# Moving the first block's residual gate into the last block, as seven products in turn between W_A and W_B

## The chip, the cores and the metric

The kernel runs on one core of a Trainium2 chip. The metric is the device time of one execution in microseconds; the median of three runs before the change is 2507.09 us (2506.99 to 2508.43).

## What is computed

One layer of a hybrid sequence model over 2048 prompt tokens and 64 sample tokens, width 1024, all in float32. What matters for this change is the end of the layer; the reference cut to it:

```python
merged = jax.nn.sigmoid(gA) * yA + jax.nn.sigmoid(gB) * yB      # yA = a @ w_a_out, yB = o @ w_b_out
out = jnp.einsum('btd,de->bte', merged, w_o)
x = x + rms_norm(out, g_post)
gate = jax.nn.sigmoid(jnp.einsum('btd,de->bte', rms_norm(x, g_ple), w_ple_gate))
x = x + jnp.einsum('btp,pd->btd', p.astype(x.dtype), w_ple_proj) * gate
```

In the kernel `h` is `rms_norm(x, g_ple)`, `p` is the product with `w_ple_proj`, and the last two lines are "the gate" or W_G.

## The kernel before

The tokens lie along the free dimension, in three blocks of 768, 704 and 640 tokens (`SIZES`, line 35); the width of 1024 is 8 tiles of 128 partitions. A block runs through `path_b` (attention heads), `path_a` (a gated convolution), and then four square products with 1024 x 1024 weights: W_A, W_B, W_O and W_G (line 33). Between W_O and W_G stands the normalization `final_norm` (line 1420).

**Three matmuls for one.** Each operand is split into a rounded part `hi` and the rest `lo` (`split`, line 229: ScalarE casts, VectorE subtracts), and each product is hi x hi + hi x lo + lo x hi (lines 457 to 459, 608 to 610, 645 to 647).

**Plain products.** `gemm` (line 652) makes one output tile from 8 k in two halves of the tokens, 24 matmuls each half. `final_gate` (line 1497) does W_G so for the first and the second block: 8 outputs; for each it asks for x and p from DRAM (`reload`), takes the sigmoid on ScalarE, multiplies and adds on VectorE, and stores y.

**Seven products in turn.** `in_turn` (line 573) makes a square product from 2 x 2 quarters with seven products in place of eight (`IN_TURN`, line 84). The quarters of the weights are A11, A12, A22 and the sums S1 to S4; those of the operand are B11, B21, B22 and the sums T1 to T4, made in place by VectorE (`operand_of`, line 555). Each product has four units `g` of 12 matmuls, each unit with one weight tile of 128 x 512. A unit's operand for the next product is prepared during the present one (`lead`, 1). The result of a quarter goes to a `sink`: the first column's upper quarter after A12, then after A22, S1 and S4. Before the change this form does W_A and W_O of the first block, W_A, W_B and W_O of the other two, and W_G of the last (`gate_in_turn`, line 1514).

**Weights.** `load_raw` (line 238) brings a tile of 256 KB on SP's queue, five in flight. `split_w` (line 269) splits it anew, or loads its `lo` from DRAM if an earlier use has stored it; `used_later` (line 255) says which are stored. From the second block on these stores go on POOL's queue (`stores`, line 1677). The sums S1 to S4 are made beforehand and kept in DRAM with their low parts (`prepare_sums`, line 375); those of W_G are made in the last block's `path_b`.

**Order and room.** The order of the work is that of the Python program, with weights at high priority and small steps hung between products by hand (`hooks`, `spread_out`, line 1530). `paced` (line 306) makes a DMA wait for the latest matmul. All activations live in one ring of 48 tiles in SBUF (`rt`, line 155). `keep_h` (line 1478) stores h to DRAM, and `ask_h` (line 1482) brings the second block's back during the last block's W_O, since the second block's gate runs after the last block's W_O. `merge_in_turn` (line 1360) sets up W_A and W_B in turn, with a list of what is loaded after which product.

Of the kernel before, what the change touches and what calls it, by code (L numbers as in the profile page):

```python
# [13 lines left out]
AF = mybir.ActivationFunctionType  # L14
# [80 lines left out]
def hybrid_step(  # L95
# [159 lines left out]
    def used_later(idx, part):  # L255

        if GA * 8 <= idx < GB * 8 + KB - 2:
            return part in ("S1", "S2", "S3", "S4")  # L260
        if idx in (GB * 8 + KB - 1, IV * 8):
            return part != 0 and (part != 1 or idx >= GA * 8)
        if idx < GA * 8:
            return part != 1
        if W_B <= idx < W_O:
            return part == 1 and idx - W_B >= KH
        return True
# [305 lines left out]
    def in_turn(stages, operand, lead=1):  # L573
# [5 lines left out]

        def prepare(i, k):  # L580
            if i < len(todo):
                st, n = todo[i]
                late = st["order"] is IN_TURN_LATE
                made.setdefault(i, []).append(operand_of(st["raw"], st["order"][n][1], k, late))
# [4 lines left out]
        for i, (st, n) in enumerate(todo):  # L589
            block, _, what = st["order"][n]  # L590
# [3 lines left out]
            for g in range(KH):  # L594
                i1, i2 = st["idx"] + g, st["idx"] + KH + g
                with tc.high_priority():
                    hi, lo = kept_w(i1, i2, block, block in st["anew"])
                start = what[0] != "c"
                if start:
                    other = what == "u2" and st["order"] is IN_TURN_LATE  # L600
                    st["bank"][g] = [ps_attn()[:, : hn()] if other else ps_gemm(), st["bank"].get(g)]
                ps, held = st["bank"][g]
                if what == "u2":
                    st["bank"][g] = held
                add = partial(T.matmul, ps, skip_group_check=not start)
                for k in range(KH):
                    xhi, xlo = xs[k]
                    add(hi[:, k, :], xhi, start=start and k == 0, stop=False)  # L608
                    add(hi[:, k, :], xlo, start=False, stop=False)  # L609
                    last[0] = add(lo[:, k, :], xhi, start=False, stop=k == KH - 1).ins  # L610
                if what == "p1":
                    st["mid"].append(rt())
                    with tc.high_priority():
                        A.copy(half(st["mid"][g], 0), ps)
                u2, p57 = half(st["mid"][g], 0), half(st["mid"][g], 1)
                if what == "c11":
                    st["sink"](g, 0, 0, ps, None)
                elif what == "u2":
                    V.tensor_tensor(u2, u2, ps, ALU.add)
                elif what == "c21":  # L620
                    st["sink"](g, 1, 0, u2, ps)
                elif what == "c12":
                    st["sink"](g, 0, 1, u2, ps)
                elif what in ("p5", "p7") and g not in st["other"]:
                    st["other"].add(g)
                    with tc.high_priority():
                        A.copy(p57, ps)
                elif what in ("p5", "p7"):
                    t = hf()
                    with tc.high_priority():  # L630
                        A.copy(t, ps)
                    V.tensor_tensor(p57, p57, t, ALU.add)
                    st["sink"](g, 1, 1, u2, p57)
# [726 lines left out]
    def merge_in_turn(a, kept, mg, first):  # L1360


        ob, m = [], []

# [11 lines left out]
        def loads(idx, n):  # L1376
# [4 lines left out]
                (W_A, 3): ("o", ob),  # L1381
                (W_A, 5): ("o", ob),
                (W_A, 6): (GB, mg),
                (W_B, 1): (GB, mg),
            }.get((idx, n), (None, m))
            if kind is not None:
# [449 lines left out]
```

## Time and profile before

| | us |
|---|---|
| median of 3 runs | 2507.09 |
| lowest, highest | 2506.99, 2508.43 |
| profiled execution: span | 2509.2 |
| first block's gate (L645 to L647, 128 x 384) | 959.6 to 1026.7 |
| last block: W_A, W_B, W_O in turn (L608 to L610) | 2222.1 to 2374.2 |
| second block's gate, with the last block's product of p | 2374.2 to 2452.7 |
| last block's gate in turn | 2452.7 to 2502.3 |

The span runs from the first to the last instruction of the one profiled execution; no other time is given for that execution. The stretches are read from the starts of the matmuls by line and number of columns. PE is TensorE's matmuls, PEld its weight loads, DVE is VectorE, ACT is ScalarE, POOL is GpSimd, whose queue issues the DMAs of activations (q0), and SP is SyncE, whose queue issues those of weights (q1).

### The profile page before, as it was taken

Reading aid. Unit: us, or ns where it says so; the run is one execution under the profiler, and the core shown is the slowest. Engines: PE = TensorE matmul, PEld = TensorE weight load, DVE = VectorE, ACT = ScalarE, POOL = GpSimd, SP = SyncE. Lnnn points to the kernel's source line nnn. Section 1 sums busy time; section 2 is a strip of 40 time slices with the busy share of each in tenths; the row PEclk is TensorE's granted clock in tenths of the full one; section 3 lists DMA queues with packets and bytes.
Section 4 is the critical chain, followed back from the end, with each engine's and each line's share of the span. In section 5 each row is a group of like instructions: output and inputs, shape, how many; then the busy total and the mean of one; then the engine's idle time right before and its main releaser. Section 6 shows DMA issues by size and latency. Waiting matters only on the chain.

```text
span 2509.2 us, 47311 instructions
## 1 busy us (share of the span) xinstructions
PE 2491.1 (99%) x16254; PEld 2474.0 (99%) x16254; DVE 1932.2 (77%) x3699; ACT 1503.9 (60%) x2926; POOL 513.9 (20%) x875
## 2 busy tenths in 40 slices
PE   9999999999999999999999999999999999999998
PEld 9999999999999999999999999999999999999998
DVE  7889999988868775588886657977677776678766
ACT  6676676554453664466655556576666655565646
POOL 2032223321022021122223211102122222111031
PEclk9999999999999999999999999999999999999999
DMA  8789888997697798788889988979988879889887
GB/s 330 241 302 336 320 297 318 331 321 271 229 339 259 250 329 295 258 270 287 283 278 332 337 293 307 327 266 357 349 284 289 278 257 313 297 274 337 294 302 259
DMA packets 344240, 746.14 MB, mean 297 GB/s; under 512 B 43318, under 2 KB 48496, under 8 KB 344000
## 3 DMA queue, kind: packets, MB, share of 16 engines
q1 hardware_dynamic: 287136, 519.96, 60.3%
q0 software_dynamic: 56864, 223.16, 25.1%
q8 instruction: 128, 2.10, 0.3%
q14 instruction: 112, 0.92, 0.1%
HBM read 530.59 MB, written 212.36 MB: 296 GB/s over the span
## 4 chain that ended last, share of the span: by engine, by line
PE 90%; DMA 3%; DVE 3%; ACT 2%; issue 1%; POOL 0%; SPq 0%; ACTq 0%; DVEq 0%; POOLq 0%
PE pg L457 20%; PE pg L458 19%; PE pg L459 19%; PE pg L609 5%; PE pg L608 5%; PE pg L610 5%; PE pg L646 3%; PE pg L647 3%; PE pg L645 3%; DMA raw<-S 2%; PE pa L1142 1%; PE pa L1110 1%; PE pa L1180 1%; PE pa L1182 1%; DMA raw<-w_blk 1%
## 5 line engine op out<-in xcount | busy, mean ns | idle before, releaser
L457 PE MATMUL pg<-r,hi 128*128 128x320 f32 (+2 forms) x3304 | 1074.7, 325 | 1.1 <-DVE r L505 1.1
L458 PE MATMUL pg<-r,hi 128*128 128x320 f32 (+2 forms) x3304 | 1066.8, 323 | 0.0
L459 PE MATMUL pg<-r,lo 128*128 128x384 f32 (+2 forms) x2380 | 775.3, 326 | 0.4 <-DMA lo<-low 0.4
L457 PEld LDWEIGHTS pg<-r,hi 128*128 128x128 f32 x3304 | 621.0, 188 | 3.5 <-DVE r L505 1.7
L458 PEld LDWEIGHTS pg<-r,hi 128*128 128x128 f32 x3304 | 621.6, 188 | 0.0
L279 ACT CAST hi<-raw 128x512 fp32r<-128x512 f32 x566 | 349.9, 620 | 415.4 <-PE pg L458 170.6
L459 PEld LDWEIGHTS pg<-r,lo 128*128 128x128 f32 x2380 | 447.1, 188 | 0.7 <-DMA lo<-low 0.7
L230 ACT CAST hi<-raw 128x512 fp32r<-128x512 f32 x404 | 249.5, 621 | 206.3 <-PE pg L458 83.8
L609 PE MATMUL pg<-r,hi 128*128 128x320 f32 (+2 forms) x976 | 312.1, 321 | 2.5 <-DVE r L230 2.5
L608 PE MATMUL pg<-r,hi 128*128 128x320 f32 (+2 forms) x976 | 309.8, 320 | 0.0
L459 PE MATMUL pg<-r,s 128*128 128x352 f32 (+1 forms) x924 | 291.4, 315 | 0.0
L230 DVE TENSOR_TENSOR lo<-raw,hi 128x512 fp32r<-128x512 f32 x304 | 208.1, 686 | 82.7 <-ACT hi L230 75.9
L230 DVE TENSOR_TENSOR r<-r,r 128x320 fp32r<-128x320 f32 (+7 forms) x374 | 220.2, 608 | 46.1 <-ACT r L230 44.9
L230 ACT CAST r<-r 128x320 fp32r<-128x320 f32 (+7 forms) x374 | 195.9, 557 | 35.0 <-DVE r L1353 9.0
L610 PE MATMUL pg<-r,lo 128*128 128x320 f32 (+2 forms) x640 | 204.2, 319 | 0.1
L609 PEld LDWEIGHTS pg<-r,hi 128*128 128x128 f32 x976 | 183.2, 188 | 4.6 <-DVE r L230 4.3
L608 PEld LDWEIGHTS pg<-r,hi 128*128 128x128 f32 x976 | 182.3, 188 | 1.4 <-ACT r L230 1.0
L230 ACT CAST hi<-s 128x512 fp32r<-128x512 f32 x164 | 101.9, 623 | 127.3 <-PE pg L458 97.0
L459 PEld LDWEIGHTS pg<-r,s 128*128 128x128 f32 x924 | 173.5, 188 | 0.0
L471 ACT COPY hf<-pg 128x352 f32<-128x352 f32 (+2 forms) x354 | 157.5, 448 | 0.8 <-PE pg L459 0.7
L230 DVE TENSOR_TENSOR lo<-s,hi 128x512 fp32r<-128x512 f32 x164 | 114.2, 696 | 45.6 <-ACT hi L230 43.1
L505 DVE TENSOR_TENSOR r<-hf,pg 128x128 f32<-128x128 f32 (+5 forms) x164 | 64.3, 411 | 98.7 <-PE pg L459 98.6
(389 smaller groups left out, 4223.4 us busy)
## 6 DMA issues: line engine op xcount, KB each, us to landing
raw<-w_blk SPq DMA_DIRECT2D x559, 256.0 KB, 4.6
raw<-S SPq DMA_DIRECT2D x452, 256.0 KB, 4.2
lo<-low SPq DMA_DIRECT2D x340, 256.0 KB, 4.4
s<-low SPq DMA_DIRECT2D x226, 256.0 KB, 5.1
low<-lo SPq DMA_DIRECT2D x207, 256.0 KB, 3.9
S<-s SPq DMA_DIRECT2D x152, 256.0 KB, 4.2
low<-r POOLq DMA_DIRECT2D x66, 256.0 KB, 4.5
r<-w_blk POOLq DMA_DIRECT2D x64, 256.0 KB, 6.7
```

Source lines behind the costliest of these rows:

```text
L230: return A.copy(hi, src).ins, V.tensor_tensor(lo, src, hi.bitcast(F32), ALU.subtract).ins
L279: A.copy(hi, raw)
L457: add(hi[:, k, :], xhi, start=start and k == 0, stop=False)
L458: add(hi[:, k, :], xlo, start=False, stop=False)
L459: last[0] = add(lo[:, k, :], xhi, start=False, stop=k == KH - 1).ins
L471: copied = A.copy(got[n], ps[bank])
L608: add(hi[:, k, :], xhi, start=start and k == 0, stop=False)
L609: add(hi[:, k, :], xlo, start=False, stop=False)
L610: last[0] = add(lo[:, k, :], xhi, start=False, stop=k == KH - 1).ins
L645: T.matmul(ps, hi[:, k % 4, :], xhi[:, c], start=k == ks[0], stop=False)
L646: T.matmul(ps, hi[:, k % 4, :], xlo[:, c], start=False, stop=False)
L647: last[0] = T.matmul(ps, lo[:, k % 4, :], xhi[:, c], start=False, stop=k == ks[-1]).ins
```

## The change

The first block no longer runs `final_gate`. Its h goes to DRAM as the second block's does (`keep_h`, and 0 for `early` in `final_norm`). A new stage `earlier_gate` stands in the last block's list of stages, between W_A and W_B, with the first block's width of 768 (`as_of`). Its h is asked for after the fourth and sixth product of W_A, its p and x as half tiles four places ahead, and what W_B loads after products of W_A is now loaded after those of the new stage. `used_later` leaves out the low part of W_G's A21, which only the second block's plain gate uses. The body of the loop in `in_turn` has become the function `unit`, without other change. The core of the diff:

```diff
@@ used_later
+        if idx >= W_G + KH:
+            return part == 1
         return True
@@ in_turn
+        def as_of(st):
+            return sized_to(st["bl"]) if "bl" in st else nullcontext()
...
-                made.setdefault(i, []).append(operand_of(st["raw"], st["order"][n][1], k, late))
+                with as_of(st):
+                    made.setdefault(i, []).append(operand_of(st["raw"], st["order"][n][1], k, late))
...
+                with as_of(st):
+                    unit(st, n, g, xs)
@@ merge_in_turn
-    def merge_in_turn(a, kept, mg, first):
+    def merge_in_turn(a, kept, mg, first, between=None):
+        by = W_G if between else W_A
...
-                (W_A, 3): ("o", ob),
-                (W_A, 5): ("o", ob),
-                (W_A, 6): (GB, mg),
+                (by, 3): ("o", ob),
+                (by, 5): ("o", ob),
+                (by, 6): (GB, mg),
...
+            if between and idx == W_A and n in (3, 5):
+                between["ask"]()
+            if between and (idx, n) == (W_A, 6):
+                between["terms"](4)
...
             dict(idx=W_A, order=IN_TURN, raw=a, sink=sink_a, anew=("A11", "A12")),
+            *([between] if between else []),
             dict(idx=W_B, order=IN_TURN, raw=ob, sink=sink_b, anew=("A11", "A12")),
@@ new
+    def earlier_gate(bl, kept):
+        h, asked = [], []
+        places = iter([(g, c, q) for c, q in ((0, 0), (1, 0), (1, 1), (0, 1)) for g in range(KH)])
+
+        def ask():
+            with sized_to(bl):
+                for j in range(len(h), len(h) + KH):
+                    h.append(reload(kept["h", j], True))
+
+        def ask_terms(n):
+            with sized_to(bl):
+                for g, c, q in islice(places, n):
+                    t = rt()
+                    for o, kind in enumerate("px"):
+                        paced(G.dma_start(half(t, o), half(kept[kind, g + c * KH], q)))
+                    asked.append(t)
+
+        def sink(g, c, q, x, y):
+            j, t, s = g + c * KH, asked.pop(0), whole(x, y)
+            if y is None:
+                s = hf()
+                A.activation(s, x, AF.Sigmoid)
+            else:
+                A.activation(s, s, AF.Sigmoid)
+            v = half(t, 0)
+            V.tensor_tensor(v, v, s, ALU.mult)
+            V.tensor_tensor(v, v, half(t, 1), ALU.add)
+            G.dma_start(y_fm[j * P : (j + 1) * P, bl["t0"] + q * hn() : bl["t0"] + (q + 1) * hn()], v)
+            ask_terms(1)
+
+        return dict(idx=W_G, order=IN_TURN, raw=h, anew=(), sink=sink, bl=bl, ask=ask, terms=ask_terms)
@@ main loop
+        between = earlier_gate(blocks[0], kepts[0]) if bl["last"] else None
+        before, loads, ob, m = merge_in_turn(a, kept, mg, first, between)
...
-            norm = sized(bl, final_norm(bl, xo, kept, partial(split_h, h2) if first else partial(keep_h, kept), int(first)))
+            norm = sized(bl, final_norm(bl, xo, kept, partial(keep_h, kept), 0))
...
-            if first:
-                run(final_gate(bl, h2, kept))
-            else:
+            if not first:
```

More of the change, by code (lines that the diff above doesn't have):

```diff
@@ L589, in in_turn @@
         for i, (st, n) in enumerate(todo):
-            block, _, what = st["order"][n]
             if n == 0:
@@ L594, in in_turn @@
             for g in range(KH):
[L595 to L633, printed above, removed]
+                with as_of(st):
+                    unit(st, n, g, xs)
                 if lead > 1 or i > 0:
@@ L1473, in final_norm @@
             yield
-    def split_h(h2, j, t):
-        h2.append(split_rt(t))
     def keep_h(kept, j, t):
@@ L1733, in hybrid_step @@
         stages = [out_in_turn(mg, xo, bl["last"])]
-        before, loads, ob, m = merge_in_turn(a, kept, mg, first)
+        between = earlier_gate(blocks[0], kepts[0]) if bl["last"] else None
+        before, loads, ob, m = merge_in_turn(a, kept, mg, first, between)
         loads(W_A, -1)
```

41 lines of the change are left out of this document (added).

## The prediction

> **What bounds the kernel now.** I read the page first, then stretches of the span (busy time by engine), then the transfers, the waits and the chain of waits of the stretches that the edit touches.
>
> ```profile
> span 2509.2 us, 47311 instructions
> PE 2491.1 (99%) x16254; PEld 2474.0 (99%) x16254; DVE 1932.2 (77%) x3699; ACT 1503.9 (60%) x2926; POOL 513.9 (20%) x875
> ```
>
> TensorE is busy 99% of the span, so time goes down only if matmuls go, and goes up wherever TensorE is made to wait. No other time of the profiled execution is listed than its span, 2509.2, which is 2.1 us (0.08%) above the median 2507.09. I work out a difference inside the span and add it to the median.
>
> The next fence is the view of stretches. The columns after the length are busy time of PE, PEld, DVE, ACT and POOL, then granted clock, DMA share, GB/s.
>
> ```profile
> core 0: us, PE busy (x) PEld busy (x) DVE busy (x) ACT busy (x) POOL busy (x), PEclk, DMA share, GB/s
> 720.00:740.00 20.00, 20.00 (x117) 20.00 (x115) 17.29 (x34) 10.66 (x21) 9.40 (x18) 1.00 1.02 390
> 861.70:959.60 97.90, 97.51 (x615) 97.12 (x614) 72.42 (x107) 65.55 (x116) 17.96 (x30) 1.00 0.88 311
> 959.60:1026.70 67.10, 67.10 (x385) 67.10 (x384) 29.82 (x39) 19.15 (x35) 13.51 (x25) 1.00 0.83 269
> 1680.50:1780.00 99.50, 97.43 (x669) 96.91 (x668) 66.30 (x106) 63.70 (x120) 23.43 (x40) 1.00 0.94 347
> 1750.00:1800.00 50.00, 50.00 (x342) 50.00 (x342) 29.61 (x54) 31.33 (x58) 9.38 (x17) 1.00 0.99 371
> 1760.00:1780.00 20.00, 20.00 (x138) 20.00 (x137) 10.42 (x18) 10.97 (x22) 5.05 (x10) 1.00 1.04 409
> 2222.10:2271.80 49.70, 49.70 (x341) 49.70 (x340) 35.63 (x80) 31.68 (x69) 6.37 (x12) 1.00 0.91 321
> 2271.80:2324.40 52.60, 50.54 (x337) 49.16 (x336) 46.27 (x107) 30.98 (x69) 4.26 (x8) 1.00 0.90 311
> ```
>
> 959.6 to 1026.7 is the first block's gate, 2222.1 to 2271.8 the last block's W_A, and 2271.8 to 2324.4 its W_B. The clock is 1.00 throughout. The gate is an easy stretch: VectorE is busy 30 of 67 us and the transfers run at 269 GB/s. The place to which it moves is not: W_A and W_B there run at a DMA share of 0.9. The kernel's best rates are 409 GB/s over 20 us and 371 over 50.
>
> ```profile
> PEld pg L609 <- DVE r L230: 2.8, 3, 1.2
> ```
>
> This is the first row of TensorE's waits from 2222 to 2325, all three of them where W_B begins. The chain of waits there, in order of time (start, length, what), names what came late:
>
> ```profile
> 2265.66 8.62 DMA raw<-w_blk
> ...
> 2276.12 0.41 DVE r L230
> ```
>
> A weight tile took 8.6 us to land; its split stands on VectorE ahead of the operand (the last row) for which TensorE waited. So the last block's stages already lose 2.8 us to transfers at 321 GB/s. That sets the question: how many bytes does the moved gate bring to this place?
>
> **Part 1, matmuls removed.** The gate of the first block is 8 outputs x 2 halves x 8 k x 3 = 384 matmuls of 384 columns. By seven products it is 7 x 4 x 4 x 3 = 336 of the same width.
>
> ```profile
> L645 PE MATMUL pg<-r,hi x128: 334/336/340, 959.6 to 1026.2; 128*128 128x384 f32 x128
> L608 PE MATMUL pg<-r,hi x112: 331/337/342, 676.8 to 735.1; 128*128 128x384 f32 x112
> ```
>
> The rows give one of three matmuls each. A matmul is shown as 336 ns, but they overlap, so the row that counts is the stretch: 67.1 / 384 = 175 ns each. The first block's own W_A (second row, 336 matmuls up to where the next stage starts, 735.6) took 58.8 us, again 175 ns. So TensorE alone would give 58.8 - 67.1 = -8.3 us. The gate's stretch has no wait to be saved inside it.
>
> **Part 2, bytes of the moved gate.** The removed stretch:
>
> ```profile
> DMA packets 6533, 18.06 MB, mean 269 GB/s; under 512 B 912, under 2 KB 912, under 8 KB 6528
> ...
> raw<-w_blk SPq DMA_DIRECT2D x16, 256.0 KB, 3.4
> low<-lo SPq DMA_DIRECT2D x13, 256.0 KB, 3.1
> r<-x POOLq DMA_DIRECT2D x8, 384.0 KB, 4.7
> r<-p POOLq DMA_DIRECT2D x8, 384.0 KB, 5.3
> y_fm<-r POOLq DMA_DIRECT2D x7, 384.0 KB, 4.5
> ```
>
> By the code it is 16 weight tiles, 16 low parts stored and 24 tiles of 384 KB: 17,408 KB = 17.8 MB, against 18.06 MB measured, so counting by the code works. The last block's W_A:
>
> ```profile
> DMA packets 7547, 15.95 MB, mean 321 GB/s; under 512 B 911, under 2 KB 911, under 8 KB 7541
> ...
> raw<-S SPq DMA_DIRECT2D x16, 256.0 KB, 4.5
> raw<-w_blk SPq DMA_DIRECT2D x12, 256.0 KB, 6.7
> ...
> r<-o POOLq DMA_DIRECT2D x8, 320.0 KB, 6.9
> ```
>
> The new stage loads the same 28 weight tiles (7,168 KB). The low parts of the 16 sums are loaded (4,096). Those of A11, A12 and A22 are not in DRAM yet, so they are split anew and stored (12 x 256 = 3,072). The terms p and x come as 32 half tiles of 192 KB (6,144; the first 8 are asked for as W_A ends and land in this stage), y goes out in 16 halves (3,072), and the 8 o tiles of W_B are asked for here (2,560). That is 26,112 KB = 26.74 MB; the last four halves of y (0.79 MB) may land in W_B, which leaves 25.95 MB. In 58.8 us this needs 441 GB/s, above any rate in the rows. TensorE would have to wait:
> - at 409 GB/s the stage takes 63.4 us;
> - at 390 (720 to 740) 66.5 us;
> - at 371 69.9 us;
> - at 321, the rate at which W_A ran with a wait behind it, 80.8 us.
>
> I take 390: it is the rate of 20 saturated us in a stage of the same kind (a W_A), where TensorE did not wait. The bursts (A22 and S1, with terms, y and o) have calmer products S2 and S3 between, which speaks against 409 throughout.
>
> **Part 3, the other engines in that stage.** VectorE's split of an operand of 384 columns, from the groups of the whole span:
>
> ```profile
> L230 DVE TENSOR_TENSOR r<-r,r 128x384 fp32r<-128x384 f32 x60 | 31.6, 552 | 9.9 <-ACT r L230 9.9
> ```
>
> The split of a weight tile and an issue on POOL's queue, from the groups of the removed stretch:
>
> ```profile
> L230 DVE TENSOR_TENSOR lo<-raw,hi 128x512 fp32r<-128x512 f32 x13 | 9.0, 692 | 25.9 <-ACT hi L230 22.1 <-DMA raw<-w_blk 3.8
> ...
> L1339 POOL DMA_DIRECT2D r<-x x8 | 4.3, 540 | 34.3 <-DMA y_fm<-r 28.9 <-DMA g__2915_12134<-r 5.2 <-DVE hf L498 0.3
> ```
>
> VectorE: 28 splits of operands, 16 sums for T2, 8 additions of products, 12 in whole, 32 of sigmoid's product and x: 96 x 0.552 = 53.0, and 12 weight splits x 0.692 = 8.3, together 61.3 us if none overlap. Scaled by width from W_B's measured 46.27 it is 46.27 x 384/320 = 55.5. Against 58.8 of TensorE it is nearly a second bound, but behind the 66.5 of the transfers it is hidden. POOL, at 0.54 an issue: while c21 and c22 are made (8 units, 16.8 us) it issues 8 y, 16 terms, 4 low parts and 4 o, 32 x 0.54 = 17.3 us, so its queue is just full. A store of y waits there for VectorE, and the terms for four units later (8.4 us), low parts and o stand behind it. This pulls the same way as the bytes and is not counted twice.
>
> **Part 4, the edges.** W_A loads 8 h of 384 KB in place of 8 o of 320: +0.5 MB, 1.3 us at 390; it had little room, so I take +1.0 (bounds 0 and 1.3). The 2.8 us wait then stands ahead of the new stage instead of ahead of W_B: no change. In the first block's normalization h is now stored, 8 x 384 KB = 3.1 MB, which takes 861.7 to 959.6 from 311 to 343 GB/s, while x is stored earlier. The second block's same stretch, at 347, shows what that costs:
>
> ```profile
> PEld pa L722 <- issue: 1.5, 1, 1.5
> PEld pg L457 <- DVE r L505: 1.0, 1, 1.0
> ```
>
> That is 2.5 us; the first block's own had one wait of this kind:
>
> ```profile
> PEld pg L457 <- DVE r L505: 0.7, 1, 0.7
> ```
>
> The bounds are 0 and 1.8; I take 0.7, nearer to none, because the matmuls around it are longer (352 columns, not 320). A wait of 0.7 us just behind the gate may go; I count 0 (bound -0.7). The four A21 tiles that the second block's gate now splits anew replace loads of their low parts: nothing. Fewer tiles stay in the ring after the first block; TensorE did not wait for that, so nothing.
>
> **Sum:** -67.1 + 66.5 + 1.0 + 0.7 = +1.1 us, 2507.09 + 1.1 = 2508.2. A measurement of this kernel can tell 0.2% (5.0 us) from no change, so this is no change, 2502.1 to 2512.1. With the forecast's own bounds (63.4 to 69.9, edges -0.7 to 3.1) it is 2502.7 to 2513.0.
>
> **Rivals.** *The transfers fit* (0.22). Prefetched weights, the gaps in W_A and the calmer W_B take up the excess. The stage then takes 58.8 to 60: -8.3 to -7.1 and an edge of up to 1, 2498.8 to 2501. For it: 409 GB/s beside an unhindered TensorE. Against it: the 8.6 us landing at only 321. It decides from 430 GB/s upward (stage under 60.4).
>
> [...]
>
> *The weights starve* (0.28; slower). When both queues are full, POOL's long packets take most of the DMA engines:
>
> ```profile
> q0 software_dynamic: 1228, 5.03, 64.3%
> q1 hardware_dynamic: 1501, 2.73, 37.5%
> ```
>
> From 720 to 740 POOL's queue (q0) moved 5.03 MB and the weights (q1) 2.73, or 137 GB/s, enough for a stage with its weights in hand, but S1 and S4 need 8 tiles of 256 KB each per product of 8.4 us (58.8 / 7), 250 GB/s. TensorE then waits for weights and the calm products cannot pay back. At 321 GB/s the stage takes 80.8 us: +15.4, 2522.5. It is slower by over 0.2% from a stage of 70.4 us up, 369 GB/s and less. [...]
>
> *VectorE binds* (0.05): 61.3 + 1.7 - 67.1 = -4.1, 2503.0, no change. *The edit does not do what it says* needs no chance: the matmul count is fixed by the loops.
>
> **How the numbers follow.** Forecast 0.45, all within 0.2% but its edge. Faster 0.22, within 0.2% 0.50, slower 0.28. The range 2500 to 2519 leaves out the far end of the starving (0.12) and the best of the fit (0.07).
>
> **What would show it.** Right: no matmuls of the plain gate after 960; a stage of 336 matmuls of 384 columns between the last block's W_A and W_B, some 66 us long, at 380 GB/s or more, with TensorE waiting on splits behind late weights or terms in the products A22, S1 and S4. Wrong: that stage at 59 to 60 us without waits (the fit), or over 71 us with low and raw landing in over 10 us (starving); or TensorE waiting on VectorE while transfers are under 350 GB/s.

## The result, and the profile after

The changed kernel takes 2523.45 us (median of 4 runs, 2519.06 to 2524.82), the kernel before, beside it on the same chip, 2507.04 (4 runs, 2505.88 to 2508.43). The ratio is 1.0062, 95% interval 1.005 to 1.0075: slower by 0.6%, three times what a measurement can tell. The profiled execution took 2524.27 us, its span is 2522.6: 13.4 us more than the span before (the medians lie 16.4 apart). Of all the executions below one was slow, one of the eleven of experiment e13 (3789.76 us at a granted clock of 0.597), and it counts in no ratio.

The page, its first lines:

```profile
span 2522.6 us, 47483 instructions
PE 2491.5 (99%) x16206; PEld 2470.0 (98%) x16206; DVE 1955.7 (78%) x3771; ACT 1521.6 (60%) x2970; POOL 542.4 (22%) x927
```

48 matmuls are gone, as the change says, and TensorE is nonetheless busy as long as before (2491.1). So its matmuls have become longer somewhere, and it stands still for some 13 us more. The stretches, read from the starts of the matmuls, tell where. (The 336 matmuls of W_A in the kernel before run from 2222.1 to 2271.4, so W_A ends there and not at 2271.8; W_B's 336 end at 2324.1.)

| us | before | after | difference |
|---|---|---|---|
| first block's gate, then the new stage | 67.1 | 68.2 | +1.1 |
| last block's W_A | 49.3 | 49.2 | -0.1 |
| last block's W_B and W_O | 102.8 | 107.8 | +5.0 |
| second block's gate, with the product of p | 78.5 | 85.3 | +6.8 |
| last block's gate | 49.7 | 49.7 | 0 |
| second block from its start (861.7, changed 861.5) to its W_A, without the moved gate | 587.2 | 588.6 | +1.4 |
| its three products in turn; last block to W_A | 706.0 | 706.8 | +0.8 |

Ahead of the second block and behind the last matmul together it is 1.7 us less. The moved gate itself costs what it cost; the time is lost in two stretches behind it. One caution: a stage ends in this table where the next one's first matmul starts. W_B's first matmul starts 2.35 us after the new stage's last, where 0.17 is the usual step, so 2.2 of the 68.2 us are a wait for W_B's first operand. The stage's own time is 66.1 us, and W_B with W_O, this wait included, takes 110.0, 7.2 more than before.

The view of stretches, as before: us, PE, PEld, DVE, ACT, POOL, granted clock, DMA share, GB/s. The rows are W_A, the new stage, the first 15.6 us of W_B, and the first block's normalization with the second block's beginning:

```profile
2157.00:2206.20 49.20, 49.20 (x338) 49.20 (x337) 36.55 (x81) 31.75 (x69) 7.46 (x14) 1.00 0.94 334
2206.20:2274.40 68.20, 61.30 (x337) 57.95 (x336) 49.62 (x100) 39.02 (x80) 32.81 (x61) 1.00 0.99 367
2274.40:2290.00 15.60, 12.61 (x59) 11.28 (x60) 14.03 (x30) 8.52 (x20) 4.85 (x9) 0.78 1.01 386
...
861.70:959.60 97.90, 97.09 (x612) 96.70 (x611) 66.93 (x101) 61.17 (x110) 21.18 (x36) 1.00 0.91 328
```

The new stage has its 336 matmuls in 68.2 us, with the DMA engines busy 0.99 of it. In the third row the granted clock, 1.00 in all the stretches that the prediction quoted, is 0.78: in 15.6 us TensorE made 59 matmuls, where at W_A's pace (49.2 / 336 = 0.146 us each) 106 would fit. The last row has the stores of h in it and lost 0.4 us of TensorE.

The transfers of the new stage (the row of GB/s is its 40 slices of 1.7 us), and then those of 2265 to 2285, across the seam to W_B:

```profile
GB/s 360 374 413 398 411 393 390 408 385 416 396 393 406 396 400 402 186 309 284 357 215 213 314 291 318 277 382 416 413 389 400 396 392 384 416 389 393 400 404 396
DMA packets 10374, 25.02 MB, mean 367 GB/s; under 512 B 1650, under 2 KB 1650, under 8 KB 10368
...
q0 software_dynamic: 4171, 13.66, 51.2%
q1 hardware_dynamic: 6197, 11.29, 47.3%
...
raw<-S SPq DMA_DIRECT2D x16, 256.0 KB, 8.4
raw<-w_blk SPq DMA_DIRECT2D x13, 256.0 KB, 10.9
r<-p POOLq DMA_DIRECT2D x16, 192.0 KB, 6.3
...
y_fm<-r POOLq DMA_DIRECT2D x11, 192.0 KB, 5.9
```

```profile
q0 software_dynamic: 1453, 5.11, 64.7%
q1 hardware_dynamic: 1587, 2.88, 38.6%
...
raw<-w_blk SPq DMA_DIRECT2D x4, 256.0 KB, 11.0
```

The stage moved 25.02 MB, at about 400 GB/s but for ten slices in its middle, the calm products. Weights that took 4.5 us (sums) and 6.7 us in W_A before take 8.4 and 10.9 us. Across the seam POOL's queue moves 256 GB/s (5.11 MB in 20 us) and the weights get 144: the shares that the prediction had read from 720 to 740, now where they hurt.

TensorE's longest waits in the new stage, then the longest of W_B's beginning (2274 to 2330):

```profile
PEld pg L609 <- DMA lo<-low: 5.5, 5, 2.5
PEld pg L608 <- DVE r L230: 1.9, 3, 1.3
```

```profile
PEld pg L607 <- ACT r L230: 6.0, 3, 2.3
```

In the stage a low part from DRAM is late (L609 is the product with it). In W_B the operand is late: ScalarE's cast of `split` (L230). The first of these waits (2.3) is the one that the table counts in the stage. The chain of waits there, in order of time, says what held it:

```profile
2266.07 7.38 DMA r<-p
...
2275.08 5.12 DMA y_fm<-r
2280.25 0.56 DVE r L1571
...
2281.10 4.97 DMA y_fm<-r
2286.10 0.45 ACT r L230
```

It runs through the gate's own terms and stores, and ends in the casts for which TensorE waited up to 2286.6. A cast writes a tile of the ring, and the chain puts a store that has not yet landed ahead of it: room in the ring may be what is late.

**The second gate.** TensorE's waits from 2382 to 2467, where there were none before, and the chain behind the one that is there:

```profile
PEld pa L720 <- POOL cols L712: 4.5, 1, 4.5
```

```profile
2440.69 0.54 POOL y_fm L1524
2441.23 0.54 POOL r L1349
2441.77 5.35 DMA r<-p
2447.21 0.90 DVE r L1522
2448.14 0.89 DVE r L1523
2449.03 0.94 DVE cols L733 x2
...
2451.94 0.26 POOL cols L712
2452.24 1.54 PE pa L720 x6
2453.78 0.27 PE pa L1323
```

These are the last outputs of the second block's gate and the last block's normalization, which overlap. On POOL's queue two stores of y stand in a row (2435.32 and 2440.69) and the loads of the next x and p behind the second (2441.22, 2441.77); before, each pair of loads was issued directly behind one store (the last at 2433.15 and 2433.69, behind the store of 2432.61). So p lands late, VectorE waits for it at L1522, and the column sums of the normalization (L733) stand behind that on VectorE's queue. POOL's step at L712 follows, and for that TensorE waited (L720). The program text of this gate did not change, though by `used_later` it now splits four weight tiles anew (VectorE has 73 instructions in it, 69 before). The order on the queue differs between the two kernels all the same, and the trace doesn't say why.

**The clock.** The last row of that chain shows matmuls of 0.27 us that took 0.15 us elsewhere. The stretches around two such pieces:

```profile
2272.98:2276.40 3.42, 1.26 (x7) 0.99 (x7) 2.77 (x6) 2.99 (x7) 1.42 (x3) 1.00 1.03 402
2276.40:2279.81 3.41, 3.27 (x13) 2.87 (x12) 3.41 (x9) 1.05 (x2) 2.15 (x4) 0.50 1.03 395
2447.08:2450.49 3.41, 0.95 (x7) 0.69 (x5) 3.21 (x6) 1.16 (x3) 0.78 (x2) 1.00 1.01 345
2450.49:2457.31 6.82, 5.07 (x21) 5.08 (x21) 4.41 (x6) 1.80 (x5) 2.29 (x2) 0.50 0.35 136
```

TensorE was busy for 1.26 of 3.42 us up to 2276.40, and the granted clock was 0.50 for the 3.41 us behind; it was busy for 0.95 of 3.41 us up to 2450.49, and the clock was 0.50 for 6.82 us. The records have three such pieces while the kernel works, at 2276.4, 2286.7 (3.41 each) and 2450.5 (6.83), and none in the kernel before (its one piece starts at 2505.3, behind its last matmul). TensorE was busy 3.3, 3.4 and 5.1 us in them; with 0.27 us for 0.15, at most half of that, 5.9 us, is lost to the clock (an estimate). In the second gate, 4.5 us of wait and 2.5 of half clock account for the 6.8 us.

### The profile page after: what moved, and what is told of

It is laid out like the page before. It is cut to its first block, busy times and chain, and to the rows that moved or that the text cites. A ratio compares the mean times of both kernels' runs of the same rounds, so it can differ in the third digit from the quotient of the medians.

```text
span 2522.6 us, 47483 instructions
## 1 busy us (share of the span) xinstructions
PE 2491.5 (99%) x16206; PEld 2470.0 (98%) x16206; DVE 1955.7 (78%) x3771; ACT 1521.6 (60%) x2970; POOL 542.4 (22%) x927
## 4 chain that ended last, share of the span: by engine, by line
PE 85%; DMA 5%; DVE 5%; issue 2%; ACT 2%; POOL 1%; SPq 0%; ACTq 0%; DVEq 0%; POOLq 0%
PE pg L459 19%; PE pg L461 18%; PE pg L460 18%; PE pg L608 6%; PE pg L609 6%; PE pg L607 6%; PE pg L655 2%; PE pg L657 2%; PE pg L656 2%; DMA raw<-S 1%; PE pa L1152 1%; DMA raw<-w_blk 1%; PE pa L1120 1%; PE pa L1190 1%; PE pa L1192 1%
## 5 line engine op out<-in xcount | busy, mean ns | idle before, releaser
L459 PE MATMUL pg<-r,hi 128*128 128x320 f32 (+2 forms) x3304 | 1074.9, 325 | 2.0 <-DVE r L507 2.0
L460 PE MATMUL pg<-r,hi 128*128 128x320 f32 (+2 forms) x3304 | 1066.3, 323 | 0.0
L459 PEld LDWEIGHTS pg<-r,hi 128*128 128x128 f32 x3304 | 620.8, 188 | 4.4 <-DVE r L507 2.6
L460 PEld LDWEIGHTS pg<-r,hi 128*128 128x128 f32 x3304 | 621.4, 188 | 0.0
L281 ACT CAST hi<-raw 128x512 fp32r<-128x512 f32 x578 | 357.0, 620 | 422.6 <-PE pg L460 161.8
L461 PEld LDWEIGHTS pg<-r,lo 128*128 128x128 f32 x2380 | 447.1, 188 | 1.1 <-DVE lo L230 0.8
L230 ACT CAST hi<-raw 128x512 fp32r<-128x512 f32 x404 | 249.2, 621 | 210.5 <-PE pg L460 79.3
L608 PE MATMUL pg<-r,hi 128*128 128x320 f32 (+2 forms) x1088 | 351.2, 323 | 3.4 <-DVE r L230 3.3
L607 PE MATMUL pg<-r,hi 128*128 128x320 f32 (+2 forms) x1088 | 346.5, 324 | 5.3 <-ACT r L230 5.1
L230 DVE TENSOR_TENSOR r<-r,r 128x384 fp32r<-128x384 f32 (+7 forms) x390 | 225.1, 598 | 48.9 <-ACT r L230 47.4
L230 DVE TENSOR_TENSOR lo<-raw,hi 128x512 fp32r<-128x512 f32 x304 | 208.1, 686 | 68.4 <-ACT hi L230 64.2
L609 PE MATMUL pg<-r,lo 128*128 128x320 f32 (+2 forms) x724 | 234.0, 323 | 3.9 <-DMA lo<-low 3.8
L230 ACT CAST r<-r 128x384 fp32r<-128x384 f32 (+7 forms) x390 | 200.4, 548 | 33.6 <-DVE r L1363 8.3
L607 PEld LDWEIGHTS pg<-r,hi 128*128 128x128 f32 x1088 | 204.3, 189 | 8.2 <-ACT r L230 6.9
L608 PEld LDWEIGHTS pg<-r,hi 128*128 128x128 f32 x1088 | 205.2, 189 | 6.2 <-DVE r L230 5.8
L230 ACT CAST hi<-s 128x512 fp32r<-128x512 f32 x164 | 102.0, 623 | 125.4 <-PE pg L460 103.1
L609 PEld LDWEIGHTS pg<-r,lo 128*128 128x128 f32 x724 | 136.9, 189 | 5.5 <-DMA lo<-low 5.5
L230 DVE TENSOR_TENSOR lo<-s,hi 128x512 fp32r<-128x512 f32 x164 | 113.9, 695 | 34.5 <-ACT hi L230 32.0
```

What stands on the lines that cost most here:

```text
L230: return A.copy(hi, src).ins, V.tensor_tensor(lo, src, hi.bitcast(F32), ALU.subtract).ins
L281: A.copy(hi, raw)
```

## The experiments

Two theories stood after the result. **Bytes and order:** the stage holds too many bytes, what it can't take falls on W_B, and apart from that the second gate has an unlucky order on POOL's queue. **Slots or seam:** the terms' ring tiles, or the place between W_A and W_B, hold things up, whatever the bytes. All kernels are edits of the changed kernel, but for the control e12. Each was run 4 to 11 times, beside 13 to 25 runs of the kernel before. The lengths of the stages, from one profiled execution each, with the pieces of half clock in them ("gate" is the second block's):

| | stage | W_B + W_O | gate | half clock | median | ratio to before |
|---|---|---|---|---|---|---|
| changed kernel | 68.2 | 107.8 | 85.3 | 3.4 + 3.4 + 6.8 | 2523.45 | 1.0062 [1.005, 1.0075] |
| e1 no low stores | 60.4 | 111.9 | 81.0 | 6.8 | 2515.64 | 1.0034 [1.0022, 1.0047] |
| e2 no x | 64.0 | 105.8 | 83.9 | 3.4 + 3.4 | 2519.38 | 1.0047 [1.0032, 1.0062] |
| e3 gate's terms ahead | 68.0 | 109.3 | 78.6 | 6.8 + 3.4 | 2515.93 | 1.0035 [1.0025, 1.0046] |
| e4 filled wait | 68.3 | 108.6 | 84.3 | 6.8 + 3.4 | 2520.93 | 1.0052 [1.0037, 1.0067] |
| e5 y from a half tile | 68.2 | 108.1 | 85.7 | 6.8 + 3.4 + 6.8 | 2525.31 | 1.0072 [1.0054, 1.009] |
| e7 = e1 + e3 + e5 | 60.1 | 110.9 | 78.5 | 6.8 | 2511.42 | 1.0016 [1.0007, 1.0026] |
| e9 = e3, 8 y left out | 66.2 | 111.8 | 78.5 | 6.8 + 3.4 | 2516.72 | 1.0035 [1.0022, 1.0048] |
| e10 = e3, o earlier | 69.2 | 105.1 | 78.7 | 3.4 | 2515.05 | 1.0026 [1.0015, 1.0037] |
| e13 = e1 + e10 | 62.9 | 109.2 | 78.3 | 3.4 + 3.4 | 2511.16 | 1.001 [1.0001, 1.0019] |
| e14 = e1 + e3, terms in calm products | 64.0 | 107.4 | 78.5 | 3.4 | 2507.24 | 0.9998 [0.9989, 1.0007] |

With the stage between W_B and W_O:

| | W_A + W_B | stage | W_O | half clock | median | ratio to before |
|---|---|---|---|---|---|---|
| e6 = e3, after W_B | 101.5 | 64.4 | 54.3 | 3.4 | 2513.78 | 1.0028 [1.0019, 1.0038] |
| e8 = e7, after W_B | 101.4 | 59.6 | 55.7 | 3.4 | 2509.16 | 1.0007 [0.9997, 1.0017] |
| e11 = e8, terms in calm products, without e5 | 105.0 | 60.9 | 51.1 | 3.4 + 3.4 | 2508.23 | 1.0 [0.9991, 1.0009] |

**e1, no low parts stored in the stage.**

```diff
-        return dict(idx=W_G, order=IN_TURN, raw=h, anew=(), sink=sink, bl=bl, ask=ask, terms=ask_terms)
+        return dict(idx=W_G, order=IN_TURN, raw=h, anew=("A11", "A12", "A22"), sink=sink, bl=bl, ask=ask, terms=ask_terms)
```

> The new stage splits A11, A12 and A22 anew and stores no low part (12 stores of 256 KB fewer there); the second block's gate stores them instead. Theory 1 (bytes: the stage runs at the rate that the DMA engines give, 367 GB/s measured, and the waits where W_B begins follow from the same queue): the stage moves 3.1 MB less and takes about 61 us instead of 68, W_B's beginning loses 2 to 3 us less, and the whole is 2512 to 2516. Theory 2 (POOL's queue order and slots in the ring hold the stage, not bytes): the stage stays over 66 us, since terms, y and o keep their order, and the whole stays above 2520.

3.1 MB fewer bring the stage from 68.2 to 60.4 us, 1.6 above what TensorE needs, and W_B with W_O from 107.8 to 111.9. The stores themselves are made in the second gate instead (ten of them in e7's trace), where there is room: 21.45 MB in 85 us in the changed kernel. Its waits at W_B's beginning:

```profile
PEld pg L607 <- ACT r L230: 7.4, 2, 5.8
```

One of 5.8 us, where there were three of at most 2.3. All of it now lies behind W_B's first matmul, so the table's split misleads: the stage's own time falls by 5.7 us (66.1 to 60.4), and W_B with W_O, its first wait included, rises by 1.9 (110.0 to 111.9). A third of what the stage wins is handed on. The edit takes 12 issues from POOL's queue along with the bytes.

**e2, no x.** Every half tile of x of the moved gate is left out (p is added in its place).

```diff
-                    for o, kind in enumerate("px"):
-                        paced(G.dma_start(half(t, o), half(kept[kind, g + c * KH], q)))
+                    paced(G.dma_start(half(t, 0), half(kept["p", g + c * KH], q)))
...
-            V.tensor_tensor(v, v, half(t, 1), ALU.add)
+            V.tensor_tensor(v, v, v, ALU.add)
```

> Left out: the loads of x in the new stage (16 half tiles of 192 KB, 3.1 MB); p times the gate is added to itself in place of x, so VectorE, ScalarE and the tiles of the ring are as before, and y of the first block is not the reference's. Theory 1 (bytes): the same 3.1 MB as without the low stores, so the same gain in the stage, to 61 to 62 us. Theory 2 (order and slots): the tile of the terms is still held until y has landed, so the wait where W_B begins (about 5 us with what the clock adds) stays, and the stage gains under 3 us.

The stage is 4.2 us shorter, W_B with W_O 2.0. As many bytes as in e1 are gone (with 16 issues on POOL's queue), and again the three products in turn become shorter together, by 6.2 us here and 3.7 in e1, but split differently: with the first wait counted to W_B, the stage's own time falls by 2.1 us and W_B with W_O by 4.2. Neither theory had that.

**e3, the second gate's terms asked one output ahead.**

```diff
+        terms = [(reload(kept["x", 0]), reload(kept["p", 0]))]
         for j in range(KB):
+            if j + 1 < KB:
+                terms.append((reload(kept["x", j + 1]), reload(kept["p", j + 1])))
...
-            xj, pj, t = reload(kept["x", j]), reload(kept["p", j]), rt()
+            (xj, pj), t = terms.pop(0), rt()
```

> The second block's gate asks for x and p one output earlier; nothing else changes, the new stage included. If the 4.5 us for which TensorE waited in the last normalization came from the order on POOL's queue (the loads of x and p for the seventh output issued behind the sixth store of y, so that VectorE stood at a product without its p with the column sums behind it), the wait goes, and with it the half clock behind it (6.83 us at 0.5): 2516 to 2518. If it came from the new stage's transfers still running or from the data being late altogether, the wait stays and the whole is 2522 to 2525.

The gate takes 78.6 us, as before the change; the wait and its half clock are gone. The median falls by 7.5 us. All of TensorE's waits from 2370 to 2460 in this kernel:

```profile
PEld pg L607 <- ACT r L230: 0.2, 1, 0.2
```

**e4, the wait filled.** 16 products of 128 x 128 that nobody reads stand ahead of the last normalization's transposes.

```diff
         with placed():
+            for _ in range(fill):
+                T.matmul(pb[:, :P], ident, ident, start=True, stop=True)
             for i, o in tiles_of(n):
```

> 16 matmuls of 128 x 128 that nobody reads stand ahead of the transposes for which TensorE waited 4.5 us in the last normalization; they add work only where TensorE waits. If the half clock behind that wait comes from TensorE having stood still, the clock stays at 1.00 there and the 2.3 us that it cost come back (about 2521), while the wait's cause stays. If the half clock is a matter of power or of time, it stays and the whole is 2523 to 2525, or more by the matmuls that do not fit (3 us).

The stretches where the half clock had been:

```profile
2444.00:2446.00 2.00, 0.63 (x5) 0.63 (x6) 1.97 (x5) 0.12 (x1) 0.54 (x1) 1.00 0.96 320
2446.00:2448.00 2.00, 2.00 (x20) 2.00 (x20) 1.69 (x2) 0.00 (x0) 1.92 (x1) 1.00 0.67 260
2448.00:2450.00 2.00, 2.00 (x20) 2.00 (x19) 0.00 (x0) 0.42 (x2) 0.61 (x2) 1.00 0.32 124
```

The clock stays at 1.00, with TensorE busy for 0.63 and twice 2.00 of 2 us; in the changed kernel it was busy for 0.95 of 3.41 us here, and the clock 0.50 behind that. The gate gains 1.0 us only, because the chain of waits shows the unread products (3.84 us from 2445.37, as 32 matmuls) to end last ahead of the transposes. So with the wait filled the gate's 6.83 us of half clock were gone; what sets the clock is not shown by one such run.

**e5, y from a half tile.** The sum is written to `s`, so that the terms' tile is free at once.

```diff
-            V.tensor_tensor(v, v, half(t, 1), ALU.add)
+            V.tensor_tensor(s, v, half(t, 1), ALU.add)
...
-... bl["t0"] + (q + 1) * hn()], v)
+... bl["t0"] + (q + 1) * hn()], s)
```

> In the new stage the last addition writes into the half tile of the gate, and y leaves from there, so the tile of the terms is free as soon as VectorE has added, and not only when y has landed; the transfers are the same. If the waits where W_B begins (TensorE behind ScalarE's casts of W_B's operands) come from those casts standing until a tile of the ring is free, they shrink: W_B and W_O together from 107.8 us to 103 to 105, and no half clock there, the whole 2518 to 2520. If they come from o or the weights landing late, they stay within 1 us of 107.8, or grow where the eight half tiles run out.

Stage, W_B and gate stay at 68.2, 108.1 and 85.7 us. The theory that room in the ring holds the stage falls, unless the eight half tiles that y now leaves from hold it just as long, which this run can't tell.

**e6, the stage between W_B and W_O, with e3.**

```diff
-            *([between] if between else []),
             dict(idx=W_B, order=IN_TURN, raw=ob, sink=sink_b, anew=("A11", "A12")),
+            *([between] if between else []),
```

(What W_B loads hangs on W_A's products again, and h on W_B's.)

> The stage stands between W_B and W_O in place of between W_A and W_B, with the second block's x and p asked for one output earlier (as in the run with the terms ahead, with which it is to be compared). Its loads then stand beside no load of o (2.6 MB less in the stage). Theory 1 (bytes in the stage): the stage falls from 68.0 to 61 to 64 us, and what follows it needs nothing that its queue delays: 2505 to 2510. Theory 2 (the place does not matter, since the stage starves on its own p, x and y): stage over 66 us and the whole above 2513.

The stage takes 64.4 us, and what follows it, now W_O, is 4.2 us longer than before (54.3 against 50.1). So the lateness is not W_B's own: whichever product follows pays. The place still matters in part: W_A, W_B, the stage and W_O take 220.2 us together, against 226.5 in e3 with as many bytes (76.4 and 76.5 MB); 3.0 of this is half clock, by the estimate above.

**e7, e1 and e3 and e5 together**

> Three edits together at the place of the change: no low stores in the stage, the second block's x and p one output ahead, y from a half tile. If the losses are of three separate causes that add up, stage 60.4, second gate 78.6 to 80, W_B and W_O 103 to 105: 2504 to 2508. If one waits behind another, over 2511.

The stage runs nearly at TensorE's speed and W_B waits as in e1. The transfers from 2265 to 2275 of this kernel:

```profile
DMA packets 1462, 4.05 MB, mean 405 GB/s; under 512 B 243, under 2 KB 243, under 8 KB 1461
...
q0 software_dynamic: 731, 2.71, 67.7%
q1 hardware_dynamic: 730, 1.32, 35.4%
```

The engines are full at 405 GB/s, and the weights get 132 of it, as in the changed kernel. What W_B's operand waits for can be read on ScalarE:

```profile
2279.16 0.62 ACT L230 CAST hi<-raw 128x512 fp32r<-128x512 f32 x1 [1.29 <-DMA raw<-w_blk]
2279.68 0.45 ACT L230 CAST r<-r 128x320 fp32r<-128x320 f32 x1
```

The second row is the cast that ends TensorE's wait. It stands directly behind the cast of a weight tile, which waited for the tile to land, as did the two weight casts ahead of it. The wait of 2.2 us at the seam of the changed kernel ends the same way: an operand's cast at 2273.93, behind weight casts at 2271.27 and 2272.98 that waited 1.5 and 1.1 us for their tiles.

**e8, the same after W_B**

> The same three edits with the stage between W_B and W_O. By bytes the stage then moves 21 MB where 59 us at 367 GB/s allow 21.6, so it is TensorE's alone, 59 to 60 us, and the whole -8 us against the kernel before: 2498 to 2502. If the half tiles (8) or the ring hold it, 2504 to 2510.

(The edits of e6 and e7.) The stage needs 59.6 us, 0.8 above TensorE's own, and W_O pays 5.6. At 2509.16 us the kernel can't be told from the one before.

**e9, the last eight stores of y left out, with e3.**

```diff
-            G.dma_start(y_fm[j * P : (j + 1) * P, ...
+            if (c, q) in ((0, 0), (1, 0)):
+                G.dma_start(y_fm[j * P : (j + 1) * P, ...
```

> Left out: the last 8 of the new stage's 16 stores of y (1.6 MB and 8 issues on POOL's queue in its last two products), so half of the first block's y is not written; the second block's x and p are asked for one output ahead, so it is to be compared with the run with the terms ahead (stage 68.0, W_B and W_O 109.3 us). Theory (W_B's first weight tiles land late, 11 to 14 us after issue, because POOL's long packets take two thirds of the DMA engines while its backlog drains): the backlog is 4 us shorter, raw lands in under 10 us, W_B and W_O take 104 to 106. Rival (W_B's operands stand behind VectorE's and ScalarE's own work of the last sinks, which is unchanged): 108.5 to 110.

Expected were 104 to 106 us for W_B with W_O, by the rival 108.5 to 110; it took 111.8. Here are its longest single wait, as the waits of the weight loads and then those of the matmuls have it, two stretches of W_B's beginning, and three rows from the order of time on ScalarE and VectorE:

```profile
PEld pg L607 <- issue: 4.8, 1, 4.8
```

```profile
PE pg L607 <- DVE hf L500: 4.5, 1, 4.5
```

```profile
2272.00:2274.00 2.00, 0.00 (x0) 0.00 (x0) 1.31 (x4) 1.21 (x3) 0.54 (x2) 1.00 1.03 388
...
2276.00:2278.00 2.00, 2.00 (x9) 2.00 (x9) 2.00 (x5) 0.52 (x1) 0.00 (x0) 0.50 1.04 396
```

```profile
2273.16 0.62 ACT L230 CAST hi<-raw 128x512 fp32r<-128x512 f32 x1 [0.57 <-DMA raw<-w_blk]
...
2273.81 0.69 DVE L230 TENSOR_TENSOR lo<-raw,hi 128x512 fp32r<-128x512 f32 x1 [0.69 <-ACT hi L230]
...
2274.89 0.55 DVE L500 TENSOR_TENSOR hf<-r,pg 128x384 f32<-128x384 f32 x1
```

The stores are not what fills the seam: without them 2276 to 2278 still runs at 396 GB/s. The wait of 4.8 us runs from 2270.8 to 2275.6, with a DMA share of 1.03 in its stretch from 2272 to 2274. The weight load's row names no releaser, but the matmul's does: VectorE's addition of the stage's last results (L500). That addition stands behind the split of one of W_B's weight tiles, whose cast on ScalarE waited for the tile to land. So here too the weights are late, and what stands behind their split on the two engines is late with them. The pieces of half clock, 10.2 us in all, cost up to 4.5 us here, by the same estimate.

**e10, W_B's o tiles after S2 and S3 of the stage in place of the fourth and sixth product, with e3.**

```diff
-                (by, 3): ("o", ob),
-                (by, 5): ("o", ob),
+                (by, 2 if between else 3): ("o", ob),
+                (by, 3 if between else 5): ("o", ob),
```

> The 8 o tiles are asked for after the stage's third and fourth product (S2 and S3, when POOL's queue has little to do) in place of the fourth and sixth; x and p of the second block one output ahead, so it is compared with the run with the terms ahead (68.0 and 109.3 us). The bytes are the same. Theory (POOL's backlog at the seam starves W_B's weights): 1.3 MB less at the seam, W_B and W_O 105 to 107, the stage the same or 1 us longer, the whole 2512 to 2514. Rival (the sum of bytes alone counts): stage and what follows add up to the same 177 us.

W_B with W_O fell to 105.1, the stage rose by 1.2, and the half clock moved from W_B into the stage (from 2258.3; the granted clock is 0.58 from 2258 to 2260, and 1.00 in W_B's first 15.9 us). Together that is 3.0 us less than e3, and all of it is clock: half of TensorE's busy time in the pieces is 4.7 us in e3 and 1.7 here.

**e11, the moved gate's terms four at a time in calm products, stage after W_B, with e1 and e3.**

```diff
-            ask_terms(1)
...
-            if between and (idx, n) == (W_B, 6):
+            if between and (idx, n) in ((W_B, 6), (W_G, 0), (W_G, 2), (W_G, 3)):
                 between["terms"](4)
```

> No low stores, x and p of the second block ahead, the stage between W_B and W_O, and its own terms asked for four places at a time, after W_B's last product and the stage's products A11, S2 and S3, so that in its last three products POOL's queue only stores y. Theory (backlog at the seam): W_O no longer waits for its first weights, W_O 50 to 52 us in place of 55.7, the stage 59 to 60, the whole 2500 to 2503, faster than the kernel before. Rival (the last sinks' own work holds W_O's operands): W_O stays at 55 and the whole at 2508 to 2510.

W_O came to 51.1, in the expected 50 to 52, but the whole did not come to 2500: W_A with W_B takes 3.6 us more than in e8, one piece of half clock in it, and the second block's beginning, far from the new stage, has a piece of its own (granted clock 0.79, 0.50 and 0.85 in the three stretches of 2 us from 884).

**e12, control: the kernel before, with its second gate's terms one output ahead**

(The edit of e3, for the second block alone.)

> The kernel before the change with the second block's x and p asked for one output ahead, nothing else. If the 6.8 us that the changed kernel lost in the second block's gate came from the order on POOL's queue, which the kernel before does not have, this changes nothing: 2506 to 2508. If asking ahead is a gain of its own, 2503 or less, and the run with the terms ahead said less of the order.

2508.24 us (10 runs, 2505.49 to 2510.88), ratio 1.0002 [0.9992, 1.0012]. In the kernel before this edit is worth nothing; what e3 won back was lost by the change.

**e13 and e14.** What was open by then was why W_B's beginning is late even where the stage has fewer bytes: the o tiles, the gate's own terms, or a backlog that is only pushed along. e13 joins e1, e3 and the o tiles of e10; e14 joins e1 and e3 with the terms as in e11, the stage between W_A and W_B.

> Three edits in one: A11, A12 and A22 of the moved gate load nothing and store nothing but are split on the chip each time without a store of the low part (3.1 MB fewer), the second block's gate asks for x and p one output ahead, and W_B's o tiles are asked for after S2 and S3. Theory (W_B's beginning is late because the o tiles and late weights meet in the burst S1 and S4): stage 60 to 62, W_B with W_O 104 to 107, second gate 78.6, whole 2502 to 2506, below before by 1 to 5. Rival (W_B's beginning costs the same 109 to 112 whenever the stage itself runs without waits, because the backlog is only pushed along): stage 60 to 61, W_B with W_O 109 to 112, whole 2508 to 2512.

> The same without the low stores and with the second block's terms ahead, but here the moved gate's own p and x are asked for four at a time after W_A's last product and the stage's A11, S2 and S3, not one by one behind the sinks; the o tiles stay after T-products as in the changed kernel. Theory (o tiles in the burst make W_B late): W_B with W_O stays at 108 to 112, stage 60 to 62, whole 2507 to 2511. Rival (terms and y in the burst make it late, whichever tiles they are): W_B with W_O 104 to 106, whole 2502 to 2505.

e13 has the o tiles where e10 had them, and W_B with W_O is at 109.2 all the same: the o tiles are not the cause, and e10's 105.1 was no proof of it. e14 lands between its two theories, at 107.4 with a stage of 64.0, 2 above what was expected.

The three kernels with e1's and e3's edits between W_A and W_B agree in the sum, though: stage, W_B and W_O take 171.0 (e7), 172.1 (e13) and 171.4 us (e14), against 177.3 in e3. Part of such differences is the clock. With half of TensorE's busy time in the pieces taken off, the sum is 171.5 to 172.8 us in the changed kernel, e3, e4, e5 and e10, and 168.1 to 170.4 in the five whose edits take out 3.1 MB (e1, e2, e7, e13, e14). One run does not fit: e9 leaves out 1.6 MB, and comes to 173.5. So 3.1 MB are worth 1 to 5 us here, and another order of the same requests mostly moves lateness between the stage and W_B. That it is the bytes, and not the issues on POOL's queue that go with them, no run separates; for the bytes speaks that in the changed kernel the DMA engines are busy 0.99 of the stage and POOL 32.8 of its 68.2 us. With the clock taken off and its first wait included, W_B with W_O comes to 104 to 110 us in all runs that have the stage ahead of W_B, still 1 to 7 above the 102.8 of before.

No version beats the kernel before: the best, e14, e11 and e8, can't be told from it. Their edits take back the whole loss, and TensorE's 8.3 us are still eaten up.

## Why the prediction was wrong

**Part 1 was right.** 48 matmuls fewer; with fewer bytes beside it the stage ran in 59.6 to 60.4 us (e8, e7, e1), near the 58.8.

**Part 2 was right in its sum, and one of its terms was luck.** 66.5 us were forecast (bounds 63.4 to 69.9), 68.2 measured, 66.1 of them the stage's own. The bytes were 25.02 MB, not 25.95, and the rate 367 GB/s, not 390: the 20 us from 720 to 740 were no measure for 68 us with ten slices of 1.7 us at 186 to 357. A longer measure was there. The prediction calls 371 GB/s the kernel's best over 50 us, but the same trace has 395 from 1740 to 1790, and over the stage's length

```profile
1712.00:1780.00 68.00, 66.68 (x458) 66.44 (x457) 47.48 (x76) 41.15 (x79) 17.09 (x31) 1.00 1.01 385
```

That TensorE does not set the stage is shown by e1: with 3.1 MB fewer, and the issues that go with them, its own time is 5.7 us shorter.

**Part 3 was right for VectorE**, which is busy 49.6 of 68.2 us (forecast 55.5 to 61.3) and for which TensorE waits 1.9 us.

**Part 4 failed, in three of its zeros.** The first two account for the miss: 7.2 and 6.8 us, where nothing was forecast; the other differences from the forecast come to 1.7 us the other way.
- *"The 2.8 us wait then stands ahead of the new stage instead of ahead of W_B: no change."* The stage itself makes a backlog, and W_B starts behind it. W_B with W_O is 5.0 us longer, 7.2 with the wait ahead of its first matmul, and in each run that changed the stage the product behind it was longer too. It was in sight: the rival of the starving weights rested on the very shares of the two queues, but I let it act inside the stage alone.
- *"The four A21 tiles that the second block's gate now splits anew replace loads of their low parts: nothing."* This gate was counted at nothing. It cost 6.8 us, half of the whole difference, by the order of two stores on POOL's queue (e3 takes it away, e12 shows that the order was fine before). No row of the trace before could have told which order the changed kernel would have; that it could change in a stage whose text is untouched was missing among the rivals. Whether the four splits have to do with the order, no run tells; e3 has them too and loses nothing there.
- *The clock.* All terms took 1.00, as the view of before had it. In the changed kernel it was 0.50 for 3.41 us twice and for 6.83 us once, around standstills of TensorE of 2.01, 2.06 and 4.20 us: up to 5.9 of the 13.4 us, which are part of the two items above.

The stores of h in the first block's normalization were counted at 0.7 and W_A at 1.0. W_A lost nothing (-0.1); the second block's part up to its W_A is 1.4 us longer, of which the stretch 861.7 to 959.6 shows 0.4 as standstill. The second lies within the spread of that part from run to run (586.4 to 591.6 us among the experiments).

**The rivals.** The starving weights named 2522.5, and 2523.45 was measured, but not by that way: it wanted 80.8 us for the stage at 321 GB/s, and the stage took 68.2. Late weights are seen (raw in 10.9 us), and their price falls mostly on W_B: of the stage's waits 5.5 us are for low parts from DRAM, and W_B with W_O loses 7.2. The fit (2498.8 to 2501) was refuted by the saturated stage; yet in e1 and e7 the stage nearly was a fit, and the kernel was no faster than before.

**What stays open:** what would have to be relieved to end W_B's loss. The traces of the changed kernel, e7 and e9 put W_B's late weights ahead of its late operands, on ScalarE and VectorE; no run made the weights land sooner, so this is read from traces, not shown by a run. e7, e13 and e14 show that moving one kind of request isn't enough. Open is also why e9, with fewer bytes, is not shorter.

## What to carry to other kernels

A stage moved into a stretch whose transfers are nearly full must be costed together with the stage behind it: what the first one couldn't take in was paid by the second here (7.2 us). Here reordering the requests mostly shifted the bill, and taking bytes out paid a part of it. Read a wait at the seam from the matmuls on both sides, or it is booked to the wrong stage. Look at the granted clock around each standstill of TensorE: three of four from 2.01 to 4.20 us came with 3.41 or 6.83 us at 0.50. And look at the order on each queue in untouched stages too: it was another one here (6.8 us in the second gate), and asking for terms one step ahead took that loss away (78.6 us), and cost nothing in the kernel before (2508.24 us).

## What the runs showed of the hardware

The granted clock was 0.50 in pieces of 3.41 or 6.83 us; in the changed kernel they start at 2276.4, 2286.7 and 2450.5. TensorE's matmuls stand still there for more than 1.5 us four times. Three of these standstills have a piece behind them or across their end: 2.01 us up to 2274.4, 2.06 up to 2286.6 and 4.20 up to 2452.2. The fourth, 2.14 us from 2224.1, has none; these are the stretches around it:

```profile
2221.79:2225.20 3.41, 2.35 (x14) 2.03 (x12) 3.41 (x8) 2.73 (x6) 2.16 (x4) 1.00 1.04 401
2225.20:2228.61 3.41, 2.33 (x12) 2.06 (x12) 3.41 (x9) 0.97 (x3) 2.16 (x4) 1.00 1.03 399
2228.61:2232.02 3.41, 2.37 (x14) 2.31 (x14) 1.85 (x4) 1.71 (x5) 0.55 (x1) 1.00 1.05 400
```

TensorE was busy for 2.33 to 2.37 of 3.41 us in each of them, and the clock was 1.00. Right ahead of the three pieces it was busy for 1.26 of 3.42 us, 1.35 of 3.41 and 0.95 of 3.41. What sets the clock is not shown by so few cases. At most half of TensorE's busy time in a piece of 3.41 us, 1.7 us, was lost beside the standstill itself (the estimate from 0.27 us for 0.15).

From 2265 to 2285 in the changed kernel the DMA engines moved 401 GB/s, of which POOL's queue had 64.7% of the engines' time and the weights 144 GB/s. From 2265 to 2275 in e7 it was 405 GB/s, 67.7% and 132 GB/s.
